# First stage of a two-layer diffusion block: one of two modulation vectors moved to fp32 matmuls on TensorE, the loads in a fixed order

## Chip, core and metric

The kernel runs on one core of one Trainium2 chip. The metric is the time of one execution on the device in microseconds. Each program is timed in several runs and the median counts.

## What is computed

The reference is a two-layer block on 512 latent tokens and 256 context tokens of width 1024: SwiGLU feed-forward, attention (windowed in layer 0, differential in layer 1) and a second feed-forward, each behind an RMS norm whose scale and shift come from a conditioning vector. The part that the change touches is the first norm of layer 0, with the modulation vectors it needs, and the first projections of the first feed-forward:

```python
def _rmsnorm(x, w):
    y = xf * lax.rsqrt(jnp.mean(xf * xf, axis=-1, keepdims=True) + EPS)
    return (y * w.astype(jnp.float32)).astype(x.dtype)

def _pre(h, gain, shift, scale):
    return _rmsnorm(h, gain) * (1.0 + scale) + shift

def _swiglu(h, w_gate, w_up, w_down):
    return (jax.nn.silu(h @ w_gate) * (h @ w_up)) @ w_down
...
mx = (silu_c @ ada_w[i] + ada_b[i]).reshape(B, N_MOD, 1, D)
mc = (silu_cc @ ada_w[i] + ada_b[i]).reshape(N_MOD, D)
fx = _swiglu(_pre(hx, norm_w[i, 0], mx[:, 0], mx[:, 1]), ...)
fc = _swiglu(_pre(hc, norm_w[i, 0], mc[0], mc[1]), ...)
```

The conditioning has two streams: `c` for the latent tokens and `c_ctx` for the context tokens. Of the nine modulation vectors of layer 0, number 0 is the shift and number 1 the scale of this first norm.

## The kernel before

**Layout.** Activations stand transposed in SBUF: `hT` is 8 slices (called d, or k when they are contracted over) of 128 features by 768 tokens. Each fp32 operand of a product is split in a high and a low fp32r part, and a product is three matmuls (high by high, low by high, high by low). `xh` and `xl` are the two parts of `hT` times the scale factor; `x_parts` (L187) makes them for one slice: ScalarE writes `xh` (L193) with the factor as its scale, VectorE writes `xl` (L194), each in a piece of 256 context tokens and one of 512 latent tokens. The two last columns of `xh` and `xl` hold the shift of the two streams, so that the projections of the shift come out as two more columns of the same matmul (386 columns instead of 384) and are added later as a bias. The norm's 1/rms is not multiplied in before the projections: `rstd` is applied to their results (`scaled`, L300). So the projections need the scale, the shift columns need the shift, and nothing needs `rstd` until the results are read.

**Modulation.** A block of 128 entries of a modulation vector is a product of 128 rows of the transposed `ada_w` with the conditioning. It is done on VectorE: one scalar_tensor_tensor over 128x1024 per stream, with the sum taken out through its accumulator (`ada_junk` is its unused result). `ada_fix` (L145) then adds the bias and, for a scale, one, and multiplies the norm's weight (L152, L153; L156 for a shift). The two conditioning rows lie spread over the 128 partitions in `s_bc`.

**The first stage**, `start` (L785), makes scale and shift for the eight slices, and the first three of the 44 projection units of the feed-forward (gate 0, up 0, gate 1; 128 outputs each, 48 matmuls a unit). Per slice it loads the factor rows of the scale and of the shift (512 KB each) and the slice of `hT` (384 KB). The scale's two products run on VectorE. Of the shift's sixteen products, four run on VectorE (L826) and twelve are multiplied on GpSimd (L823) and summed on ScalarE (L824). The squares of `hT` are made on ScalarE and summed over features by fp32 matmuls with a matrix of ones (`ssq`, L178), slice by slice, into a PSUM tile of their own, from which `norm` (L228) and `rsqrt` (L211) make `rstd`. Weights of a unit come from SyncE's queue into `w_raw`, ScalarE casts the high part (L815), GpSimd subtracts the low part (L816).

**What sets the order.** A scheduler puts the instructions of each engine into one fixed sequence when the program is built, by its own estimate of times; an engine then runs its own sequence strictly in turn and waits on semaphores. SyncE's queue issues the loads; at most eight are outstanding, since each waits for the one eight before it. The projection tiles come from the PSUM pool `pffn` (name `big`), which holds four tiles. Three belong to the first units, the fourth to the squares.

**After the stage** the feed-forward goes on with its other units and, beside them, with the remaining modulation vectors of the layer: 56 "side blocks" (`ada_block`, L123, its products on L131), two products each on VectorE, their rows in the same four `w_raw` buffers as the weights.

Of the kernel before, what the change touches and what calls it, by code (L numbers as in the profile page):

```python
# [10 lines left out]
F32 = mybir.dt.float32  # L11
F32R = mybir.dt.float32r
AF = mybir.ActivationFunctionType
ALU = mybir.AluOpType
# [3 lines left out]
P = 128  # L18
D = 1024
ND = D // P  # L20
SEQ = 512
CTX = 256
T = SEQ + CTX
# [11 lines left out]
class Net:  # L35
# [141 lines left out]

    def ssq(self, d, ps):  # L178

        nc = self.nc  # L180
        sq = self.tp.tile([P, T], F32, name="ta")
        nc.scalar.activation(out=sq, in_=self.hT[:, d], func=AF.Square)
        for i in range(2):
            nc.tensor.matmul(ps[:, i, :384], self.ones, sq[:, i * 384:(i + 1) * 384], start=(d == 0),
                             stop=(d == ND - 1))
# [599 lines left out]
    def start(self, pool):  # L785

        nc, a = self.nc, self.a
        wp = self.sb("w0", 3)
        rp = self.sb("ada_first", 6)
        units = []  # L790
        for which, i in ((0, 0), (1, 0), (0, 1)):
            hi = wp.tile([P, 1024], F32R, name="w0_hi")
            lo = wp.tile([P, 1024], F32R, name="w0_lo")
            units.append((hi, lo, a["ffn_gu"][0, 0, which, i], self.pbig.tile([P, 2, 512], F32, name="big")))
        ssq = self.pbig.tile([P, 2, 512], F32, name="big")

        def load(d):
            nc.sync.dma_start(self.hT[:, d], a["xT"][:, d])
            self.ssq(d, ssq)

        for d in range(3):
            load(d)
        for d in range(ND):
            raws = []
            for c in (1, 0):
                raw = rp.tile([P, D], F32, name="ada_raw0")
                nc.sync.dma_start(raw, a["ada_w"][0, c * 8 + d])
                raws.append(raw)
            if d + 3 < ND:
                load(d + 3)  # L810
            if d < 3:
                hi, lo, src, _ = units[d]
                raw = self.rawp.tile([P, 1024], F32, name="w_raw")
                nc.sync.dma_start(raw, src)
                nc.scalar.copy(out=hi, in_=raw)  # L815
                nc.gpsimd.tensor_tensor(out=lo, in0=raw, in1=hi.bitcast(F32), op=ALU.subtract)  # L816
            for c, raw in zip((1, 0), raws):
                b = c * 8 + d
                for s in range(2):
                    acc = self.mod[:, 0, s, b:b + 1]  # L820
                    junk = pool.tile([P, D], F32, name="ada_junk")
                    if c == 0 and (s == 1 or d % 2 == 1):
                        nc.gpsimd.tensor_tensor(out=junk, in0=raw, in1=self.sbc[:, s], op=ALU.mult)  # L823
                        nc.scalar.activation(out=junk, in_=junk, func=AF.Identity, accum_out=acc)  # L824
                    else:
                        nc.vector.scalar_tensor_tensor(out=junk, in0=raw, scalar=1.0, in1=self.sbc[:, s],  # L826
                                                       op0=ALU.mult, op1=ALU.mult, accum_out=acc)
                self.ada_fix(0, b)
            self.x_parts(0, 0, d)
            b = self.mod[:, 0, :, d]  # L830
            nc.vector.tensor_copy(out=self.xh[:, d, T:], in_=b)  # L831
            nc.vector.tensor_tensor(out=self.xl[:, d, T:], in0=b, in1=self.xh[:, d, T:].bitcast(F32),  # L832
                                    op=ALU.subtract)
        view = lambda t: t.rearrange("p (k m) -> p k m", m=P)
        us = [((view(hi), view(lo)), ps) for hi, lo, _, ps in units]
        for k in range(ND):
            self.project_k(us, (k,))
        rp.release()
# [264 lines left out]
```

## Time and profile before

| | us |
|---|---|
| median of 3 runs (2902.48 to 2910.11) | 2903.91 |
| the profiled execution | 2902.44 |
| its span, from first to last instruction | 2900.6 |
| TensorE busy in the span | 2770.0 |
| VectorE busy | 1555.9 |
| ScalarE busy | 972.4 |
| GpSimd busy | 1311.2 |
| granted TensorE clock, mean | 0.982 |

Times in the profile run from the start of the span. 1.84 us of the execution's time lie outside the span. PE is TensorE, PEld its weight loads, DVE VectorE, ACT ScalarE, POOL GpSimd, SP SyncE; a q behind a name is the sequencer, which issues loads. A row of the timeline has the start, the length, the engine, the line, the operation with its tiles and shape, the number of merged instructions, and in brackets how long the engine had been idle before and what released it. An fp32 matmul leaves two records each for its weight load and its product; an fp32r one leaves one.

### The profile page before, as it was taken

Reading aid. Unit: us, or ns where it says so; the run is one execution under the profiler, and the core shown is the slowest. Engines: PE = TensorE matmul, PEld = TensorE weight load, DVE = VectorE, ACT = ScalarE, POOL = GpSimd, SP = SyncE. Lnnn points to the kernel's source line nnn. Section 1 sums busy time; section 2 is a strip of 40 time slices with the busy share of each in tenths; the row PEclk is TensorE's granted clock in tenths of the full one; section 3 lists DMA queues with packets and bytes.
Section 4 is the critical chain, followed back from the end, with each engine's and each line's share of the span. In section 5 each row is a group of like instructions: output and inputs, shape, how many; then the busy total and the mean of one; then the engine's idle time right before and its main releaser. Section 6 shows DMA issues by size and latency. Waiting matters only on the chain. (4 is left out here: it accounts for less than half of the span.)

```text
span 2900.6 us, 40961 instructions
## 1 busy us (share of the span) xinstructions
PE 2770.0 (95%) x16150; PEld 2593.4 (89%) x16150; DVE 1555.9 (54%) x2683; ACT 972.4 (34%) x1749; POOL 1311.2 (45%) x762
## 2 busy tenths in 40 slices
PE   5899999999989899999999999999989999999998
PEld 3899999989877799999998999999988887799998
DVE  7955555567887544444447333344467678522223
ACT  4322122145666421221224212221345555422223
POOL 4443343355443443333335433333465665555553
PEclk7999999999999999999999999999999999999999
DMA  6333333333242323233223232232232333233331
GB/s 240 121 112 108 125 105 118 124 115 100 82 144 81 99 78 112 76 106 117 74 90 106 75 118 84 91 120 88 85 98 74 90 89 114 83 92 100 102 105 44
DMA packets 113423, 296.38 MB, mean 102 GB/s; under 512 B 12880, under 2 KB 30928, under 8 KB 113232
## 3 DMA queue, kind: packets, MB, share of 16 engines
q1 hardware_dynamic: 112944, 293.66, 31.8%
q8 instruction: 128, 2.10, 0.3%
q14 instruction: 63, 0.52, 0.1%
q10 hardware_dynamic: 288, 0.10, 0.0%
HBM read 260.42 MB, written 15.20 MB: 95 GB/s over the span
## 5 line engine op out<-in xcount | busy, mean ns | idle before, releaser
L56 POOL TENSOR_TENSOR w_lo<-w_raw,w_hi 128x1024 fp32r<-128x1024 f32 (+2 forms) x377 | 802.1, 2128 | 1072.1 <-ACT w_hi L55 1055.6
L266 PE MATMUL big<-xh,w_hi 128*128 128x384 f32 (+3 forms) x2816 | 696.6, 328 | 38.7 <-DVE xh L831 19.5
L55 ACT CAST w_hi<-w_raw 128x1024 fp32r<-128x1024 f32 (+2 forms) x377 | 337.4, 895 | 1132.6 <-PE big L70 394.1
L266 PE MATMUL big<-xl,w_hi 128*128 128x384 f32 (+3 forms) x2816 | 693.6, 327 | 8.3 <-DVE xl L832 5.0
L266 PE MATMUL big<-xh,w_lo 128*128 128x384 f32 (+3 forms) x2816 | 693.6, 328 | 2.3 <-POOL w_lo L56 2.3
L266 PEld LDWEIGHTS big<-xh,w_hi 128*128 128x128 f32 x2816 | 502.5, 191 | 47.2 <-DVE xh L831 22.3
L266 PEld LDWEIGHTS big<-xl,w_hi 128*128 128x128 f32 x2816 | 500.3, 191 | 10.5 <-DVE xl L832 6.3
L266 PEld LDWEIGHTS big<-xh,w_lo 128*128 128x128 f32 x2816 | 497.8, 190 | 3.8 <-POOL w_lo L56 3.3
L131 DVE SCALAR_TENSOR_TENSOR ada_junk<-w_raw,s_bc 128x1024 f32<-128x1024 f32 x224 | 342.4, 1546 | 291.6 <-DMA w_raw<-ada_w 290.4
L271 DVE COPY bias<-big 128x2 f32<-128x2 f32 x176 | 27.7, 157 | 621.1 <-PE big L266 620.9
L68 PE MATMUL big<-hh,w_hi 128*128 128x512 f32 (+1 forms) x1200 | 327.6, 344 | 0.0
L70 PE MATMUL big<-hl,w_hi 128*128 128x512 f32 (+1 forms) x1200 | 327.3, 344 | 0.0
L72 PE MATMUL big<-hh,w_lo 128*128 128x512 f32 (+1 forms) x1200 | 326.8, 344 | 0.0
L311 DVE SCALAR_TENSOR_TENSOR hT<-big,mod,hT 128x512 f32<-128x512 f32 (+1 forms) x288 | 167.6, 618 | 176.7 <-PE big L72 176.4
L70 PEld LDWEIGHTS big<-hl,w_hi 128*128 128x128 f32 x1200 | 226.1, 188 | 29.5
L72 PEld LDWEIGHTS big<-hh,w_lo 128*128 128x128 f32 x1200 | 225.0, 188 | 28.6
L68 PEld LDWEIGHTS big<-hh,w_hi 128*128 128x128 f32 x1200 | 224.9, 188 | 27.2
L966 POOL TENSOR_TENSOR hl<-tb,hh 128x768 fp32r<-128x768 f32 (+1 forms) x88 | 152.3, 1730 | 183.2 <-ACT hh L965 181.9
L961 DVE SCALAR_TENSOR_TENSOR tb<-tb,bias,ta 128x512 f32<-128x512 f32 (+1 forms) x154 | 176.1, 1177 | 8.7 <-DVE tb L304 0.5
L285 PE MATMUL half<-xh,w_hi 128*128 128x384 f32 (+3 forms) x464 | 155.5, 335 | 20.6 <-DVE ta L297 18.8
L965 ACT CAST hh<-tb 128x768 fp32r<-128x768 f32 (+1 forms) x88 | 68.7, 781 | 276.5 <-DVE tb L961 276.5
L285 PE MATMUL half<-xl,w_hi 128*128 128x384 f32 (+3 forms) x464 | 153.8, 331 | 0.0
(215 smaller groups left out, 3677.6 us busy)
## 6 DMA issues: line engine op xcount, KB each, us to landing
w_raw<-ffn_gu SPq DMA_DIRECT2D x176, 512.0 KB, 3.3
w_raw<-ada_w SPq DMA_DIRECT2D x128, 512.0 KB, 3.3
w_raw<-ffn_d SPq DMA_DIRECT2D x96, 256.0 KB, 2.7
w_raw<-ffn_d SPq DMA_DIRECT2D x64, 320.0 KB, 2.9
w_raw<-diff_in SPq DMA_DIRECT2D x24, 512.0 KB, 3.2
ada_raw<-ada_w SPq DMA_DIRECT2D x16, 512.0 KB, 7.2
w_raw<-gqa_in SPq DMA_DIRECT2D x12, 512.0 KB, 3.5
og<-god SPq DMA_DIRECT2D x6, 768.0 KB, 6.5
```

Source lines behind the costliest of these rows:

```text
L55: nc.scalar.copy(out=hi[:, :cols], in_=raw[:, :cols])
L56: nc.gpsimd.tensor_tensor(out=lo[:, :cols], in0=raw[:, :cols], in1=hi[:, :cols].bitcast(F32), op=ALU.subtract)
L68: nc.tensor.matmul(o, wh, xh, start=(k == 0), stop=False)
L70: nc.tensor.matmul(o, wh, xl, start=False, stop=False)
L72: nc.tensor.matmul(o, wl, xh, start=False, stop=(k == n - 1))
L131: getattr(nc, engines[s]).scalar_tensor_tensor(out=junk, in0=raw, scalar=1.0, in1=self.sbc[:, s], op0=ALU.mult, op1=ALU.mult, accum_out=se ...
L266: mm(ps[:, c, :e - s], w[:, k], x[:, k, s:e], start=first, stop=last)
L285: mm(ps[:, :e - s], w_[:, k], x[:, k, s:e], start=(k == 0 and i == 0), stop=(k == ND - 1 and i == 2))
L311: self.nc.vector.scalar_tensor_tensor(out=h, in0=o, scalar=self.mv(l, s, c, d), in1=h, op0=ALU.mult, op1=ALU.add)
L961: nc.vector.scalar_tensor_tensor(out=u[:, tk], in0=u[:, tk], scalar=bu[:, s:s + 1], in1=g[:, tk], op0=ALU.add, op1=ALU.mult)
L965: nc.scalar.copy(out=hh[:, toks], in_=u[:, toks])
L966: nc.gpsimd.tensor_tensor(out=hl[:, toks], in0=u[:, toks], in1=hh[:, toks].bitcast(F32), op=ALU.subtract)
```

## The change

- The shift no longer uses factor rows. `ada_w`'s columns of the shift come in their natural order as a new input `ada_k` (8 pieces of 128x1024), the conditioning as a 128x16 tile `s_cp`, and sixteen fp32 matmuls on TensorE (stationary 128x2, moving 128x512) sum the shift of both streams into a PSUM tile `shift` of 2x1024. ScalarE copies it out, eight small transposes turn it to 128 features by 2, VectorE adds the bias, and `x_bias` writes the shift columns of all eight slices at once. These matmuls, and all that depends on them, stand ahead of the first projections.
- GpSimd and ScalarE no longer take part in products of the first stage; the scale's sixteen products all stay on VectorE.
- The squares go slice by slice into `acc` on VectorE (7 additions of 128x768), and `norm` makes the sum over features with its own two matmuls, into a PSUM tile that it takes from the pool, as at the other feed-forwards.
- SyncE's loads in `start` stand in the order in which they are written (`manual_schedule`); the loads of `cos`, `sin` and `final_w` land in between.
- The pool with `ada_junk` has one buffer instead of two.

```diff
-        for which, i in ((0, 0), (1, 0), (0, 1)):
...
-        ssq = self.pbig.tile([P, 2, 512], F32, name="big")
...
+        scp = op.tile([P, ND, 2], F32, name="s_cp")
+        nc.scalar.dma_start(scp, a["cond_p"])
+        nc.scalar.activation(out=scp, in_=scp, func=AF.Silu)
+        shift = self.pbig.tile([P, 2, 512], F32, name="big")
+
+        def shift_part(k):
+            raw = kp.tile([P, D], F32, name="ada_rawk")
+            nc.sync.dma_start(raw, a["ada_k"][k])
+            for i in range(2):
+                nc.tensor.matmul(shift[:2, i], scp[:, k], raw[:, i * 512:(i + 1) * 512], start=(k == 0),
+                                 stop=(k == ND - 1))
...
+        with self.tc.manual_schedule(engines={nc.sync.engine}):
+            for d in range(ND):
+                raw = rp.tile([P, D], F32, name="ada_raw0")
+                nc.sync.dma_start(raw, a["ada_w"][0, ND + d])
+                nc.sync.dma_start(self.hT[:, d], a["xT"][:, d])
+                if d < 4:
+                    shift_part(2 * d)
+                    shift_part(2 * d + 1)
+                if d in (0, 2, 4):
+                    unit(d // 2 % 2, d // 4)
+                for s in range(2):
+                    junk = pool.tile([P, D], F32, name="ada_junk")
+                    nc.vector.scalar_tensor_tensor(out=junk, in0=raw, scalar=1.0, in1=self.sbc[:, s], op0=ALU.mult,
+                                                   op1=ALU.mult, accum_out=self.mod[:, 0, s, ND + d:ND + d + 1])
+                self.ada_fix(0, ND + d)
+                self.x_parts(0, 0, d)
+                sq = self.acc if d == 0 else self.tq.tile([P, T], F32, name="sq")
+                nc.scalar.activation(out=sq, in_=self.hT[:, d], func=AF.Square)
+                if d:
+                    nc.vector.tensor_tensor(out=self.acc, in0=sq, in1=self.acc, op=ALU.add)
+        row = op.tile([2, D], F32, name="shift_row")
+        nc.scalar.copy(out=row.rearrange("p (c n) -> p c n", c=2), in_=shift[:2])
+        turned = self.pbig.tile([P, 2, 512], F32, name="big")
...
+            nc.tensor.transpose(turned[:, 0, 2 * d:2 * d + 2], row[:, d * P:(d + 1) * P], self.ident[:2, :2])
+        nc.vector.tensor_tensor(out=self.mod[:, 0, :, 0:ND],
+                                in0=turned[:, 0, :2 * ND].rearrange("p (d s) -> p s d", s=2),
+                                in1=self.ada_b[:, 0:1, 0:ND].to_broadcast([P, 2, ND]), op=ALU.add)
+        self.x_bias(0, 0)
...
-        self.adap = self.sb("ada0", 2)
+        self.adap = self.sb("ada0", 1)
```

What it moves, in the sequences as built (line numbers of the changed program in the "now" pieces are its own: L809 and L792 are the loads of the factor rows and of `ada_k`, L818 the products of the scale, L185 is `xl`, L257 the projections, L230 the norm's matmuls, L210 the first reading of their result on VectorE). First SyncE's queue at its start, before: behind three slices of `hT` come pairs of factor rows (L807), with the slices and weights in turn.

```order
L120 DMA s_bc<-cond 128x1024 x2
L798 DMA hT<-xT 128x768 x3
L807 DMA ada_raw_146<-ada_w 128x1024
L807 DMA ada_raw_148<-ada_w 128x1024 [waits DMAHW0_49]
L798 DMA hT<-xT 128x768 [waits DMAHW1_49]
L814 DMA w_raw<-ffn_gu 128x1024 [waits DMAHW2_49]
L807 DMA ada_raw_177<-ada_w 128x1024 [waits DMAHW3_49]
L807 DMA ada_raw_179<-ada_w 128x1024 [waits DMAHW4_49]
```

And the same place now:

```order
L120 DMA s_bc<-cond 128x1024 x2
L809 DMA ada_raw_133<-ada_w 128x1024
L810 DMA hT<-xT 128x768
L792 DMA ada_rawk<-ada_k 128x1024
L792 DMA ada_rawk<-ada_k 128x1024 [waits DMAHW0_49]
L801 DMA w_raw<-ffn_gu 128x1024 [waits DMAHW1_49]
L809 DMA ada_raw_162<-ada_w 128x1024 [waits DMAHW2_49]
L810 DMA hT<-xT 128x768 [waits DMAHW3_49]
```

The first factor row moved ahead of the slices, and each slice is followed by two pieces of `ada_k` until all eight are issued. Second, VectorE where `rstd` is made. Before, the norm's four steps (L219, L221, L222, L223) stand in the middle of the stage, between products and fixes of the fourth and fifth slice:

```order
L826 SCALAR_TENSOR_TENSOR ada_junk,mod<-ada_raw_240,s_bc 128x1024
L219 TENSOR_SCALAR tb<-big 128x768 [waits Activation_49]
L152 TENSOR_SCALAR mod<-mod,ada_b 128x2 [waits DVE_49]
L221 TENSOR_TENSOR tb<-tb,ta 128x768 [waits DVE_49,Activation_49]
L153 TENSOR_SCALAR mod<-mod,norm_w 128x2 [waits DVE_49]
L222 SCALAR_TENSOR_TENSOR tb<-tb,ta 128x768 [waits DVE_49]
```

Now they stand at the stage's end, behind the last piece of `xl`, seven products of side blocks (L131) and the three copies of the bias columns, which wait for TensorE to finish the three units:

```order
L185 SCALAR_TENSOR_TENSOR xl<-hT,mod,xh 128x512 [waits Activation_49]
L131 SCALAR_TENSOR_TENSOR ada_junk,mod<-w_raw,s_bc 128x1024 [waits DVE_49]
L131 SCALAR_TENSOR_TENSOR ada_junk,mod<-w_raw,s_bc 128x1024 [waits DMAHW5_49,DVE_49]
L131 SCALAR_TENSOR_TENSOR ada_junk,mod<-w_raw,s_bc 128x1024 [waits DVE_49]
L131 SCALAR_TENSOR_TENSOR ada_junk,mod<-w_raw,s_bc 128x1024 [waits DMAHW7_49,DVE_49]
L262 COPY bias<-big 128x2 [waits PE_49] x2
L131 SCALAR_TENSOR_TENSOR ada_junk,mod<-w_raw,s_bc 128x1024 [waits DVE_49]
L262 COPY bias<-big 128x2 [waits PE_49]
L131 SCALAR_TENSOR_TENSOR ada_junk,mod<-w_raw,s_bc 128x1024 [waits DMAHW1_49,DVE_49]
L131 SCALAR_TENSOR_TENSOR ada_junk,mod<-w_raw,s_bc 128x1024 [waits DVE_49]
L210 TENSOR_SCALAR tb<-big 128x768 [waits Activation_49]
```

So the reading of the norm's sum (L210) moved behind seven side products counted from the last `xl`. Third, TensorE at the end of the first three units, now:

```order
L257 MATMUL big<-xh,w_lo 128x384
L257 MATMUL big<-xh,w_lo 128x386
L230 MATMUL big<-acc,ones 128x384 [waits PE_49]
L230 MATMUL big<-acc,ones 128x384
L257 MATMUL big<-xh,w_hi 128x384 [waits DVE_49]
L257 MATMUL big<-xh,w_hi 128x386
```

The two matmuls of the norm moved to the end of the stage, and the fourth unit behind them waits for VectorE: it takes the PSUM tile that the norm's sum stood in, and the step that gives it free is L210. Before, the fourth unit took the tile of the squares, which had been read long ahead. Behind this stage the sequences of all engines are those of before but for a few neighbours exchanged.

More of the change, by code (lines that the diff above doesn't have):

```diff
@@ L176, in x_bias @@
                                 op=ALU.subtract)
[L178 to L185, printed above, removed]
     def x_parts(self, l, n, d, xonly=False):
@@ L788, in start @@
         wp = self.sb("w0", 3)
-        rp = self.sb("ada_first", 6)
-        units = []
-        for which, i in ((0, 0), (1, 0), (0, 1)):
+        rp = self.sb("ada_first", 5)
+        kp = self.sb("ada_shift", 4)
+        op = self.sb("ada_one", 1)
+        scp = op.tile([P, ND, 2], F32, name="s_cp")
+        nc.scalar.dma_start(scp, a["cond_p"])
+        nc.scalar.activation(out=scp, in_=scp, func=AF.Silu)
+        units = []
+        shift = self.pbig.tile([P, 2, 512], F32, name="big")
[5 more added lines that the diff above has]
+                                 stop=(k == ND - 1))
@@ L792, in start, with unit @@
+        def unit(which, i):
             hi = wp.tile([P, 1024], F32R, name="w0_hi")
             lo = wp.tile([P, 1024], F32R, name="w0_lo")
-            units.append((hi, lo, a["ffn_gu"][0, 0, which, i], self.pbig.tile([P, 2, 512], F32, name="big")))
-        ssq = self.pbig.tile([P, 2, 512], F32, name="big")
[L797 to L802, printed above, removed]
-        for d in range(ND):
[L804 to L833, printed above, removed]
@@ new lines, in unit @@
+            w = self.rawp.tile([P, 1024], F32, name="w_raw")
+            nc.sync.dma_start(w, a["ffn_gu"][0, 0, which, i])
+            nc.scalar.copy(out=hi, in_=w)
+            nc.gpsimd.tensor_tensor(out=lo, in0=w, in1=hi.bitcast(F32), op=ALU.subtract)
+            units.append((hi, lo, None, self.pbig.tile([P, 2, 512], F32, name="big")))
+        with self.tc.manual_schedule(engines={nc.sync.engine}):
[18 more added lines that the diff above has]
+                    nc.vector.tensor_tensor(out=self.acc, in0=sq, in1=self.acc, op=ALU.add)
@@ L837, in start @@
             self.project_k(us, (k,))
+        op.release()
+        kp.release()
         rp.release()
         wp.release()
-        return {(0, 0): us[0][1], (1, 0): us[1][1], (0, 1): us[2][1]}, ssq
+        return {(0, 0): us[0][1], (1, 0): us[1][1], (0, 1): us[2][1]}, None
     def run(self):
@@ L1069, in pack @@
         "cond": np.stack([g["c"][0], g["c_ctx"]]),
+        "cond_p": np.stack([g["c"][0], g["c_ctx"]]).reshape(2, ND, P).transpose(2, 1, 0),
+        "ada_k": g["ada_w"][0, :, :D].reshape(ND, P, D),
         "ada_w": g["ada_w"].transpose(0, 2, 1).reshape(2, 72, P, D),
```

## Prediction

> **What bounds the kernel now.** I read the page first, then the busy times stage by stage, the waits of the first 100 us, the timeline of that stretch, and the groups of instructions in it. The page:
>
> ```profile
> PE 2770.0 (95%) x16150; PEld 2593.4 (89%) x16150; DVE 1555.9 (54%) x2683; ACT 972.4 (34%) x1749; POOL 1311.2 (45%) x762
> PE   5899999999989899999999999999989999999998
> DVE  7955555567887544444447333344467678522223
> ```
>
> TensorE is the bound nearly everywhere, except in the first slices of 72.5 us each, where it shows 5 and VectorE 7 and 9. So the first stage has a limit of its own. Its windows (busy time of PE, PEld, DVE, ACT, POOL, then granted clock, DMA share, GB/s):
>
> ```profile
> 0.00:20.00 20.00, 7.33 (x17) 3.87 (x17) 7.93 (x14) 9.03 (x11) 4.76 (x8) 0.98 0.93 347
> 20.00:40.00 20.00, 11.01 (x30) 6.96 (x30) 18.09 (x20) 8.07 (x13) 13.88 (x6) 0.67 0.87 340
> 40.00:62.25 22.25, 12.05 (x45) 9.21 (x44) 16.72 (x29) 11.46 (x17) 10.42 (x5) 0.73 0.36 118
> 62.25:102.94 40.69, 30.45 (x135) 28.10 (x136) 40.23 (x61) 12.65 (x22) 17.59 (x7) 0.84 0.24 78
> 110.00:150.00 40.00, 40.00 (x229) 40.00 (x228) 31.85 (x47) 11.67 (x15) 23.42 (x9) 1.00 0.44 144
> ```
>
> From 110 us TensorE has no gap. Up to 102.94 us, where the fourth unit starts, it works 60.8 us (7.33 + 11.01 + 12.05 + 30.45), much of it at a granted clock of 0.67 to 0.84, while VectorE is full from 62 us on (40.23 of 40.69) and the loads are idle by then (0.24). Who waits for whom up to 100 us:
>
> ```profile
> ACT xh L193 <- DVE mod L153: 29.2, 7, 7.1
> POOL ada_junk L823 <- DVE ada_junk L826: 22.5, 5, 12.8
> PE big L266 <- DVE xh L831: 19.5, 6, 6.7
> PE big L266 <- DVE xl L832: 5.0, 3, 2.8
> ```
>
> TensorE waits for VectorE's shift columns, ScalarE for VectorE's scale. Why VectorE is slow shows in the timeline:
>
> ```profile
> 12.78 1.22 DVE L826 SCALAR_TENSOR_TENSOR ada_junk<-ada_raw,s_bc 128x1024 f32<-128x1024 f32 x1
> 13.93 1.22 DVE L826 SCALAR_TENSOR_TENSOR ada_junk<-ada_raw,s_bc 128x1024 f32<-128x1024 f32 x1
> 14.09 3.25 POOL L823 TENSOR_TENSOR ada_junk<-ada_raw,s_bc 128x1024 f32<-128x1024 f32 x1 [12.79 <-DVE ada_junk L826]
> 15.07 2.30 DVE L152 TENSOR_SCALAR mod<-mod,ada_b 128x2 f32<-128x2 f32 x1
> 30.77 2.38 POOL L816 TENSOR_TENSOR w_lo<-w_raw,w_hi 128x1024 fp32r<-128x1024 f32 x1 [2.45 <-ACT w_hi L815]
> 50.31 0.96 DVE L219 TENSOR_SCALAR tb<-big 128x768 f32<-128x768 f32 x1 [3.13 <-ACT ta L218]
> ```
>
> GpSimd's product and VectorE's work shut each other out: L152 has two elements per partition and takes 2.30 us, up to the end of GpSimd's instruction, which itself waited for the product before it. L219, which reads PSUM, ran 0.96 us inside such a GpSimd span. Groups up to 103 us:
>
> ```profile
> L823 POOL TENSOR_TENSOR ada_junk<-ada_raw,s_bc 128x1024 f32<-128x1024 f32 x12 | 33.5, 2801 | 38.3 <-DVE ada_junk L826 22.5 <-issue 12.0 <-ACT ta L182 2.5
> L826 DVE SCALAR_TENSOR_TENSOR ada_junk<-ada_raw,s_bc 128x1024 f32<-128x1024 f32 x20 | 31.9, 1607 | 11.9 <-DMA ada_raw<-ada_w 10.6 <-ACT ada_junk L824 1.2
> L152 DVE TENSOR_SCALAR mod<-mod,ada_b 128x2 f32<-128x2 f32 x8 | 17.0, 2130 | 0.0
> ```
>
> **The change part by part.** What counts is when the fourth unit can start; behind it TensorE is continuous and the sequences hardly change. So the sum is that start, now 102.94 us, against the new one.
>
> *Removed from GpSimd:* the twelve products of L823, 33.5 us in which VectorE mostly stands still. Three w_lo subtractions (L816) and, before the end of the stage, two of the next units stay, 2.4 us each by the row at 30.77. *VectorE* loses 4 of 20 products and 24 small instructions of the shift, and gains 7 additions.
>
> *Loads.* Their landing is read here:
>
> ```profile
> 7.32 1.06 ACT L121 ACTIVATE s_bc<-s_bc 128x1024 f32<-128x1024 f32 x1 [0.36 <-DMA s_bc<-cond]
> 11.63 1.22 DVE L826 SCALAR_TENSOR_TENSOR ada_junk<-ada_raw,s_bc 128x1024 f32<-128x1024 f32 x1 [10.63 <-DMA ada_raw<-ada_w]
> 10.00:15.00 5.00, 5.00 (x13) 2.70 (x12) 3.37 (x5) 1.81 (x3) 0.91 (x1) 1.00 1.03 407
> ```
>
> `s_bc` (1.05 MB) has landed at 7.3; three slices and the first factor row (1.70 MB more) at 11.6, so 0.39 to 0.407 MB per us; I take 0.40. Counted along the new queue: first factor row 8.6, its slice 9.6, last piece of `ada_k` 30.9, third weights 34.5, last slice 41.4. The total hardly changes: eight factor rows against eight pieces of `ada_k`. The Trainium skill (SBUF — State Buffer, summary of rules) says to reckon with about 358 GB/s between HBM and SBUF; the window's 407 speaks against so low a figure here. By 358 the last slice would land near 45 and the sum below grow by about 1 us, since VectorE comes to that slice later still.
>
> *Shift on TensorE,* sixteen fp32 matmuls of 512 columns. The nearest rows are the fp32 matmuls of 384 columns, two records each:
>
> ```profile
> 10.01 0.34 PEld L184 LDWEIGHTS big<-ta,ones 128*128 128x128 f32 x1 [0.30 <-issue]
> 10.65 0.34 PEld L184 LDWEIGHTS big<-ta,ones 128*128 128x128 f32 x1 [0.30 <-issue]
> 46.55 1.45 PE L184 MATMUL big<-ta,ones 128*128 128x384 f32 x4
> 87.77 1.97 PE L266 MATMUL big<-xh,w_hi 128*128 128x386 f32 x5 [3.26 <-DVE xh L831]
> 91.13 0.52 PE L266 MATMUL big<-xh,w_lo 128*128 128x384 f32 x2
> 91.49 0.50 PE L266 MATMUL big<-xl,w_hi 128*128 128x384 f32 x2
> 102.94 0.98 PE L266 MATMUL big<-xh,w_hi 128*128 128x384 f32 x2
> ```
>
> Slow, 0.64 us a record (10.01 to 10.65), so 1.28 a matmul and 1.71 at 512 columns; fast, 1.45/2 = 0.73, or 0.97. All sixteen cost 15.5 to 27.3 us, mostly under the loads: with the last piece at 30.9 they end between 32.9 and 38.2 (no piece overtaken by loads; all slow without a gap from 10.9). ScalarE's copy of the result stands behind `xh` of slice 3, which is not made before 35.6 (below), so up to 35.6 they cost nothing and at worst 2.6 us. No row shows the copy or the transposes: copy 1.1 us (the PSUM read at 50.31 took 0.96), eight transposes 1.5 to 6 us (a weight load each, 0.19 us by the fast rows, or four of them); I take 1.9, so 38.7. In VectorE's sequence the reading of them stands behind the products of slice 4, which end at 38.7 too.
>
> *VectorE's chain.* Prices: product 1.2 us (1.15 from 12.78 to 13.93; 1.27 where `ada_junk` has one buffer, next rows), addition 0.9, the two fixes 0.33, the two pieces of `xl` 1.13 (rows of `mod` and `xl`: medians 0.22, 0.47 to 0.74, starts overlapping), hand-over to ScalarE and back 0.8.
>
> ```profile
> L194 DVE SCALAR_TENSOR_TENSOR xl<-hT,mod,xh x16: 470/610/2840, 18.2 to 89.0; 128x256 fp32r<-128x256 f32 x8, 128x512 fp32r<-128x512 f32 x8
> L153 DVE TENSOR_SCALAR mod<-mod,norm_w x8: 215/222/2273, 17.4 to 87.6; 128x2 f32<-128x2 f32 x8
> 1561.01 0.96 DVE L208 TENSOR_TENSOR acc<-sq,acc 128x768 f32<-128x768 f32 x1 [0.57 <-ACT sq L206]
> 1563.83 1.23 DVE L131 SCALAR_TENSOR_TENSOR ada_junk<-w_raw,s_bc 128x1024 f32<-128x1024 f32 x1 [1.20 <-DMA w_raw<-ada_w]
> 1565.10 3.29 DVE L131 SCALAR_TENSOR_TENSOR ada_junk<-w_raw,s_bc 128x1024 f32<-128x1024 f32 x1
> 1573.10 1.45 PE L239 MATMUL big<-acc,ones 128*128 128x384 f32 x4
> 1574.59 0.90 ACT L218 ACTIVATE ta<-big,eps 128x768 f32<-128x768 f32 x1 [0.56 <-PE big L239]
> 1575.53 0.96 DVE L219 TENSOR_SCALAR tb<-big 128x768 f32<-128x768 f32 x1 [2.07 <-ACT ta L218]
> ```
>
> Slice 0 from 8.7 (the second row of `s_bc` is through its Silu at 7.32 + 1.06) to 13.5. Slice 1 waits for its row (14.9) and the first w_lo, to 17.1. Slices 1 to 3 take 3 x 5.6 plus the second w_lo: 36.3. Two products of slice 4: 38.7. Third w_lo: 41.1. Addition, fixes, shift columns and a product: 43.9, the low shift columns. Then eight products, three additions, eight pieces of `xl`, the fixes and two w_lo of the next units: 9.6 + 2.7 + 4.5 + 1.0 + 4.8 = 22.6, so the last `xl` at 66.5. Then seven side products, three bias copies and L210: 8.4 + 0.45 + 0.96 = 9.8, so 76.3.
>
> *TensorE beside it.* Held by the shift columns until 43.9, it has 135 of 144 matmuls left, 0.177 us each at full speed (91.13 to 91.49 for two): 68.2, or 69.7 behind the last `xl` (66.5 + 18 x 0.177). Norm 1.45 and its Ln 0.90: 72.0. VectorE arrives 4 us later: it sets the start, 76.3.
>
> *The wait that is added.* The fourth unit waits for L210, and all of TensorE's sequence behind it. Idle from 71.1 to 76.3, TensorE starts slow again: after 3.26 us idle the matmuls at 87.77 needed about 2.4 us to reach full pace, some 1.2 us lost, and the old start lost about 0.7 (102.94, 0.98 for two). I take 1 to 2 us more than before. The Trainium skill (TensorE: Matmul & The Clock Gate, Part 1) has the clock halved after an idle window of about 3.4 us and restored after as long a busy one. By it an idle of 5.2 us costs 1.7 us; the row at 87.77 recovers sooner. The units after the fourth wait for `scaled` on the first results, which needs the rest of `rstd`: L210, three products, three steps and `scaled`, about 8.6 us behind L210; the fourth unit takes 48 x 0.177 = 8.5, so that is covered to within a microsecond. One buffer for `ada_junk` costs 0.07 to 0.12 us on each of the layer's 112 side products, on an engine with 8 of 40 us free (window 110 to 150): nothing; without that cover, up to 13 us.
>
> *Sum.* 102.94 - 76.3 = 26.6, less 1.6: 25 us. The profiled execution took 2902.44 (span 2900.6 and 1.84 outside): 2877.4. The median of the runs was 1.5 above it, so 2903.9 - 25 = 2879. A measurement of this kernel can tell about 0.3% (8.7 us) from no change.
>
> **The rivals.**
>
> *TensorE bounds the stage.* If VectorE is held up less (a w_lo slipping in where it is idle, side products not in the way of L210), the start is TensorE's: from 40 us 144 matmuls with a slow start, 68, norm, Ln and L210: 71. Gain 31 to 37. For it: VectorE's slack exists in slices 0 and 1. Against: the seven side products stand ahead of L210 in the sequence.
>
> *VectorE is held up more.* The 27 products cost 1.6 instead of 1.2, as the mean of L826 (1607 ns) with all its lock-outs: 11 us more, gain 14, or 10 to 19. For it: GpSimd still has five w_lo. Against: twelve of its instructions are gone.
>
> *TensorE stays slow.* Fed in small pieces it would do the 135 matmuls at half pace (0.32): from 46 to 90, the fourth unit at 95, gain 7. For it: granted clocks of 0.67 to 0.84 up to 102 us, with gaps. Against: from 44 us on four slices are ready and more come faster than they are used; from 110 on the clock is 1.00. The Trainium skill's page on TensorE (HAM oscillation) describes bursts that never get warm because each wait is longer than the window.
>
> *The shift's matmuls are the bound, and it gets slower.* All first projections stand behind them. At p us per matmul they end at 10.9 + 16p, and the fourth unit starts some 40 us later (copy, transposes, shift columns, 25.6 us of matmuls at full pace, norm). This passes 102.94 at p = 3.3 and loses over 8.7 us from p = 3.8 on; at 4 it gives 115, so 2916. For it: no row shows a 2-column stationary with a 512-column fp32 stream. Against: the columns streamed set the nearest rows, and they give 0.97 to 1.71.
>
> *It is given back later.* The gain stays if the rest is bound by TensorE at the same pace; a rest that waits elsewhere for VectorE or loads could eat it. Busy 9 in nearly all slices speaks against. Time 2901 to 2904.
>
> **How the numbers follow.** Forecast (gain 19 to 31) 0.60; TensorE bounds 0.14; VectorE held up more 0.13; slow TensorE 0.05; given back 0.03; shift bound 0.05. The range leaves out the last two and the slow end of the slow TensorE: gains of 38 to 11, 2866 to 2893. Faster by over 0.3%: 0.60 + 0.14 + 0.13 and half of the slow case, 0.90; same 0.05; slower 0.05.
>
> **What would show it.** Right: no GpSimd product in the first stage, L152 at 0.22 us; last shift matmul between 33 and 38 us; last `xl` near 66; one gap of TensorE of about 5 us ended by L210; the fourth unit's start near 76; from there no gap. Wrong: shift matmuls over 2 us each; gaps of TensorE waiting for each slice; a granted clock near 0.5 from 45 to 70 us; a later stage longer than before.

## The result and the profile after

| | before | changed |
|---|---|---|
| median of 4 runs, us | 2903.2 (2902.48 to 2910.11) | 2885.31 (2883.55 to 2886.75) |
| ratio, 95% interval | 1 | 0.9938 (0.9926 to 0.9951) |
| profiled execution, us | 2902.44 | 2884.58 |
| its span, us | 2900.6 | 2882.8 |

Faster by 17.9 us, where 25 was forecast. The page of the changed kernel, same lines as shown of before:

```profile
PE 2765.0 (96%) x16162; PEld 2583.7 (90%) x16162; DVE 1523.9 (53%) x2661; ACT 962.3 (33%) x1727; POOL 1274.4 (44%) x750
PE   6999999999998899999999999999989999999998
DVE  8645455567886744445446333334468677522223
```

TensorE's second slice (72 to 144 us) went from 8 to 9 tenths, its first from 5 to 6. The windows of the first stage (columns as before: PE, PEld, DVE, ACT, POOL, granted clock, DMA share, GB/s):

```profile
0.00:20.00 20.00, 9.27 (x16) 1.43 (x16) 9.84 (x17) 7.46 (x9) 3.05 (x7) 1.00 0.91 345
20.00:40.00 20.00, 10.77 (x28) 2.42 (x27) 17.71 (x27) 8.35 (x12) 5.81 (x2) 0.90 1.03 407
40.00:62.25 22.25, 21.13 (x107) 21.13 (x108) 22.25 (x41) 7.75 (x12) 3.58 (x2) 0.86 0.34 126
62.25:83.25 21.00, 17.68 (x88) 16.80 (x87) 20.86 (x34) 7.89 (x9) 2.39 (x1) 0.92 0.59 181
```

GpSimd's busy time from 0 to 62 us fell from 29.06 to 12.44 us, and from 40 to 62 us TensorE is nearly full (21.13 of 22.25 us). The groups of instructions up to 83 us:

```profile
L818 DVE SCALAR_TENSOR_TENSOR ada_junk<-ada_raw,s_bc 128x1024 f32<-128x1024 f32 x16 | 23.6, 1476 | 8.6 <-DMA ada_raw<-ada_w 8.4
L794 PE MATMUL big<-ada_rawk,s_cp 128*2 128x512 f32 x32 | 18.4, 730 | 15.9 <-DMA ada_rawk<-ada_k 15.8
L152 DVE TENSOR_SCALAR mod<-mod,ada_b 128x2 f32<-128x2 f32 x8 | 1.8, 224 | 0.0
```

L152, eight instructions of two elements per partition, fell from 17.0 us to 1.8. The shift costs TensorE 18.4 us (two records a matmul). The chain in order of time, rows chosen from the timeline:

```profile
8.36 1.22 DVE L818 SCALAR_TENSOR_TENSOR ada_junk<-ada_raw,s_bc 128x1024 f32<-128x1024 f32 x1 [7.36 <-DMA ada_raw<-ada_w]
...
29.03 5.29 PE L794 MATMUL big<-ada_rawk,s_cp 128*2 128x512 f32 x8 [2.51 <-DMA ada_rawk<-ada_k]
34.55 0.98 ACT L827 COPY shift_row<-big 2x1024 f32<-2x1024 f32 x1
35.68 0.62 PE L830 MATMUL big<-ident,shift_row 2*128 2x2 f32 x8 [1.36 <-ACT shift_row L827]
37.30 2.73 POOL L803 TENSOR_TENSOR w_lo<-w_raw,w_hi 128x1024 fp32r<-128x1024 f32 x1 [6.17 <-ACT w_hi L802]
37.76 0.17 DVE L831 TENSOR_TENSOR mod<-big,ada_b 128x16 f32<-128x16 f32 x1
40.90 0.16 DVE L174 CAST xh<-mod 128x16 fp32r<-128x16 f32 x1
41.12 0.69 PE L257 MATMUL big<-xh,w_hi 128*128 128x386 f32 x1 [3.40 <-DVE xh L174]
42.30 0.17 DVE L175 TENSOR_TENSOR xl<-mod,xh 128x16 fp32r<-128x16 f32 x1
...
60.66 0.74 DVE L185 SCALAR_TENSOR_TENSOR xl<-hT,mod,xh 128x512 fp32r<-128x512 f32 x1
65.11 3.32 DVE L131 SCALAR_TENSOR_TENSOR ada_junk<-w_raw,s_bc 128x1024 f32<-128x1024 f32 x1
68.41 1.45 PE L230 MATMUL big<-acc,ones 128*128 128x384 f32 x4
72.18 0.95 DVE L210 TENSOR_SCALAR tb<-big 128x768 f32<-128x768 f32 x1
73.19 0.81 PE L257 MATMUL big<-xh,w_hi 128*128 128x384 f32 x2 [3.32 <-DVE tb L210]
```

TensorE gets the shift columns at 41 us and runs without a gap to the norm; the one gap behind it, 3.32 us, is ended by L210, and the fourth unit starts at 73.19.

That row must not be set against before's row at 102.94. The projection matmuls of before up to 102.9 us, by form:

```profile
L266 PE MATMUL big<-xh,w_hi 128*128 128x386 f32 x32 | 13.3, 428 | 19.5 <-DVE xh L831 19.5
...
L266 PE MATMUL big<-xh,w_hi 128*128 128x384 f32 x32 | 11.3, 404 | 6.0 <-ACT xh L193 6.0
```

Six forms with 32 each are 192 matmuls, four units of 48. Before had woven the fourth unit into its first stage, and at 102.94 the **fifth** starts. The changed kernel starts its fifth unit (its 193rd matmul) at 83.25: 19.7 us earlier. The gain at later places, from the first matmul of the norm there: 22.3 us at the attention block's norm (639.5 against 617.2), 16.6 at the next norm behind that block (1006.1 against 989.5), 17.8 at the end.

### The profile page after: what moved, and what is told of

Same layout as the page of the kernel before. It is cut to its first block, busy times and chain, and to the rows that moved or that the text cites. A ratio compares the mean times of both kernels' runs of the same rounds, so it can differ in the third digit from the quotient of the medians.

```text
span 2882.8 us, 40921 instructions
## 1 busy us (share of the span) xinstructions
PE 2765.0 (96%) x16162; PEld 2583.7 (90%) x16162; DVE 1523.9 (53%) x2661; ACT 962.3 (33%) x1727; POOL 1274.4 (44%) x750
## 5 line engine op out<-in xcount | busy, mean ns | idle before, releaser
L257 PE MATMUL big<-xh,w_hi 128*128 128x384 f32 (+3 forms) x2816 | 691.9, 327 | 22.4 <-DVE hT L302 13.1
L257 PE MATMUL big<-xl,w_hi 128*128 128x384 f32 (+3 forms) x2816 | 689.4, 326 | 3.3 <-DVE xl L185 3.2
L257 PE MATMUL big<-xh,w_lo 128*128 128x384 f32 (+3 forms) x2816 | 690.9, 327 | 0.4 <-POOL w_lo L56 0.4
L257 PEld LDWEIGHTS big<-xh,w_hi 128*128 128x128 f32 x2816 | 501.0, 191 | 26.7 <-ACT sq L197 11.1
L257 PEld LDWEIGHTS big<-xl,w_hi 128*128 128x128 f32 x2816 | 498.7, 190 | 4.1 <-DVE xl L185 4.1
L257 PEld LDWEIGHTS big<-xh,w_lo 128*128 128x128 f32 x2816 | 496.9, 190 | 0.8 <-POOL w_lo L56 0.8
L131 DVE SCALAR_TENSOR_TENSOR ada_junk<-w_raw,s_bc 128x1024 f32<-128x1024 f32 x224 | 330.1, 1474 | 304.5 <-DMA w_raw<-ada_w 302.3
```

Of the source, the lines that this page charges most:

```text
L131: getattr(nc, engines[s]).scalar_tensor_tensor(out=junk, in0=raw, scalar=1.0, in1=self.sbc[:, s], op0=ALU.mult, op1=ALU.mult, accum_out=se ...
L257: mm(ps[:, c, :e - s], w[:, k], x[:, k, s:e], start=first, stop=last)
```

## The experiments

The theories. **A:** GpSimd's twelve products shut VectorE out, and taking them away is the gain. **B:** it is the fixed order of loads. **C:** it is that TensorE makes all shift columns at once. Then the price of the wait for L210, and where 5.7 us went between two norms.

"Fifth unit" is the start of the 193rd projection matmul in the profiled run; "block" the stretch from the attention block's norm to the next norm; the ratio is to before on the same chip.

| run | fifth unit, us | block, us | span, us | median, us | ratio (95%) |
|---|---|---|---|---|---|
| before | 102.94 | 366.6 | 2900.6 | 2903.2 | 1 |
| changed | 83.25 | 372.3 | 2882.8 | 2885.31 | 0.9938 (0.9926 to 0.9951) |
| e1 before, fixed loads | 102.41 | 370.0 | 2901.9 | 2906.46 | 1.0024 (1.0015 to 1.0033) |
| e2 before, VectorE only | 86.29 | 370.9 | 2886.2 | 2890.66 | 0.9973 (0.9963 to 0.9983) |
| e3 both of these | 84.80 | 373.7 | 2892.2 | 2888.80 | 0.9965 (0.9953 to 0.9978) |
| e4 changed, free loads | 93.74 | 370.8 | 2891.9 | 2894.98 | 0.9983 (0.9974 to 0.9991) |
| e5 changed again | 83.03 | 372.7 | 2883.3 | 2886.63 | 0.9944 (0.9931 to 0.9956) |
| e6 changed, GpSimd products added | 108.34 | 369.9 | 2904.6 | 2908.07 | 1.0025 (1.0016 to 1.0034) |
| e7 changed, norm ahead | 78.43 | 369.3 | 2876.2 | 2879.34 | 0.9924 (0.9911 to 0.9938) |
| e8 changed, x tokens first | 83.75 | 359.7 | 2870.1 | 2872.04 | 0.9902 (0.9888 to 0.9915) |
| e9 e7 and e8 | 78.14 | 359.1 | 2869.8 | 2870.52 | 0.9892 (0.9877 to 0.9908) |
| e10 changed, shift twice | 86.51 | 373.8 | 2888.5 | 2887.86 | 0.9954 (0.9942 to 0.9967) |
| e11 e2 with x tokens first | 87.64 | 360.3 | 2879.8 | 2877.70 | 0.9920 (0.9907 to 0.9934) |
| e12 before, x tokens first | 102.25 | 357.8 | 2892.2 | 2895.18 | 0.9983 (0.9974 to 0.9992) |

In the comparisons of e1 to e12 before's median was 2900.1 to 2901.4. The two profiles of the changed kernel (changed, e5) differ by 0.2 us at the fifth unit and 0.5 at the end, so a stage can be read from one profile, as far as this one pair tells; single whole executions differ by more (e3's profiled run ended 8.4 us before before's, its median 11.3 below).

**e1.** The first stage of before with its loads in program order.

```
+        with self.tc.manual_schedule(engines={nc.sync.engine}):
             for d in range(3):
                 load(d)
             for d in range(ND):
...
```

> The kernel before with one edit: SyncE's loads of the first stage stand in program order; all else is left to the scheduler. Theory A (the gain comes from taking GpSimd's twelve products away, which shut VectorE out): the loads were idle from 62 us on while VectorE was full, so nothing much changes: time within 4 us of before (2899 to 2907), GpSimd's products still 33 us in sum, the scale fix L152's mean still about 2.1 us. Theory B (the gain comes from the order of the loads): 9 to 18 us faster than before (2885 to 2894). Theory C (the gain comes from having all shift columns at once from TensorE): no change either, as by A.

The stage is as it was (102.41), GpSimd's products take 34.1 us in sum and L152 2062 ns, as A had it. The time is 6.3 us (0.24%) longer, more than the 4 that A allowed; in the profiled run 3.4 us went in the attention block. By itself, the order of loads gives before nothing; B falls for the old kernel.

**e2.** All 32 products of the old stage on VectorE.

```
-                    if c == 0 and (s == 1 or d % 2 == 1):
+                    if False:
```

> The kernel before with one edit: the twelve products that GpSimd made (and ScalarE summed) are made on VectorE like the other twenty; the shift still comes from natural weights, loads by the scheduler. Theory A: VectorE takes on 12 x 1.2 = 14.4 us and is no longer shut out for 33.5 us of GpSimd products; of these about two thirds counted, so 8 us faster (4 to 14: 2889 to 2899), L152 at 0.22 us. Theory B: no change (within 4 us). Theory C: TensorE still gets its shift columns slice by slice, behind 32 products of VectorE instead of 20, so 0 to 14 us slower.

Groups up to 103 us of this run:

```profile
L826 DVE SCALAR_TENSOR_TENSOR ada_junk<-ada_raw,s_bc 128x1024 f32<-128x1024 f32 x32 | 38.3, 1213 | 10.3 <-DMA ada_raw<-ada_w 10.3
L152 DVE TENSOR_SCALAR mod<-mod,ada_b 128x2 f32<-128x2 f32 x8 | 1.7, 216 | 0.0
```

VectorE makes twelve products more and is done earlier: they cost 38.3 - 31.9 = 6.4 us, and L152 alone gives 15.3 back. The fifth unit starts 16.7 us earlier, 85% of the change's 19.7, by one line. A holds, and was even too modest for the stage; C falls. The whole gains less than the stage: 7.8 us by the ratio (0.9973), 9.5 by the medians, 14.4 by the spans of the profiled runs; its executions lie between 2887.55 and 2895.85. In the profiled run 4.3 us went in the attention block.

**e3.** Both edits.

> The kernel before with both edits: all products on VectorE, and SyncE's loads in program order. Theory A: as the run with the first edit alone, within 4 us of it. Theory B: as the run with fixed loads alone, 9 to 18 us faster than before. Theory C: 0 to 14 us slower than before.

The fifth unit comes 1.5 us earlier than in e2; the ratios of e2 and e3 can't be told apart. As A had it.

**e4.** The changed kernel, loads left to the scheduler.

```
-        with self.tc.manual_schedule(engines={nc.sync.engine}):
-            for d in range(ND):
+        for d in range(ND):
...
```

> The changed kernel with one edit: SyncE's loads are left to the scheduler. Theories A and C: within 4 us of the changed kernel (2881 to 2889). Theory B: the gain is lost, 2894 to 2904.

Here B is right and A and C are wrong. SyncE's queue, the shift's matmuls and ScalarE's copy in this run, rows chosen:

```profile
20.42 2.88 SPq L809 DMA_DIRECT2D hT<-xT  x3
24.00 0.33 SPq L792 DMA_DIRECT2D ada_rawk<-ada_k  x1
25.24 0.33 SPq L106 DMA_DIRECT2D cos<-cos  x1
...
28.79 1.34 SPq L126 DMA_DIRECT2D w_raw<-ada_w  x2
30.78 0.33 SPq L792 DMA_DIRECT2D ada_rawk<-ada_k  x1
33.03 3.57 PE L794 MATMUL big<-ada_rawk,s_cp 128*2 128x512 f32 x4 [12.52 <-DMA ada_rawk<-ada_k]
33.05 1.00 SPq L792 DMA_DIRECT2D ada_rawk<-ada_k  x2
38.29 6.97 PE L794 MATMUL big<-ada_rawk,s_cp 128*2 128x512 f32 x12 [1.69 <-DMA ada_rawk<-ada_k]
...
50.50 0.98 ACT L826 COPY shift_row<-big 2x1024 f32<-2x1024 f32 x1
```

The scheduler puts four pieces of `ada_k` behind three token slices; three of them also behind `cos`, `sin`, `final_w` and two factor rows of a later stage. The last shift matmul ends at 45.3 instead of 34.3, the copy stands at 50.5 instead of 34.55, the fifth unit starts 10.5 us later. The time lies in B's range and keeps 0.17% against before. So the order of loads is no gain of its own, but a condition of the new shift: with the shift on TensorE, all first projections stand behind the last piece.

**e5.** The changed kernel unedited.

> The changed kernel once more, unedited, as the comparison for the three runs beside it. All theories: ratio to before 0.993 to 0.995, the fifth unit at 82 to 84 us of its profile.

As expected: 83.03, 0.9944.

**e6.** GpSimd's products given back.

```
+                    if s == 1 or d % 2 == 1:
+                        dum = op.tile([P, D], F32, name="ada_dummy")
+                        nc.gpsimd.tensor_tensor(out=dum, in0=raw, in1=self.sbc[:, s], op=ALU.mult)
-        kp = self.sb("ada_shift", 4)
+        kp = self.sb("ada_shift", 3)
```

> The changed kernel with twelve GpSimd products of 128x1024 added (each factor row times the same broadcast rows, into a tile that nobody reads; one buffer less for the pieces of ada_k). It gives back GpSimd's share of the old first stage and nothing else. Theory A (these products shut VectorE out): about 12 x 2.8 = 33 us of GpSimd work return, of which about half falls on VectorE's path, so the fifth unit starts 10 to 22 us later than in the changed kernel (93 to 105) and the time is 10 to 20 us longer. Theory C (the gain is the shift columns from TensorE): VectorE is slower but TensorE is fed from 41 to 46 us on as before, so at most 5 us longer.

The groups up to 103 us:

```profile
L822 POOL TENSOR_TENSOR ada_dummy<-ada_raw,s_bc 128x1024 f32<-128x1024 f32 x12 | 35.1, 2926 | 7.5 <-DMA ada_raw<-ada_w 6.9
L818 DVE SCALAR_TENSOR_TENSOR ada_junk<-ada_raw,s_bc 128x1024 f32<-128x1024 f32 x16 | 27.7, 1728 | 7.4 <-DMA ada_raw<-ada_w 7.1
L152 DVE TENSOR_SCALAR mod<-mod,ada_b 128x2 f32<-128x2 f32 x8 | 8.0, 1000 | 0.0
```

And from the timeline the last matmuls of the shift and the copy of it on ScalarE:

```profile
28.80 3.60 PE L794 MATMUL big<-ada_rawk,s_cp 128*2 128x512 f32 x8 [2.51 <-DMA ada_rawk<-ada_k]
47.91 0.98 ACT L830 COPY shift_row<-big 2x1024 f32<-2x1024 f32 x1
```

The products' results are used nowhere, yet the fifth unit comes 25.1 us later and the time is 21 us longer (2908.07 against 2886.63 beside it): slower than before. L152 and L818 are long again, and through ScalarE's queue even the copy of the shift, which VectorE does not make, comes 13 us later. Above A's 10 to 22, far above C's 5. Two other causes fall by these rows: the buffer that the edit takes from `ada_k` did not hold the shift up, since its matmuls end at 32.4 us here and at 34.3 without the products, and L818 waits for loads 7.1 us in all, not more than the 8.4 there. The copy stands behind an `xh` that waits 11.2 us for VectorE's L153. With e2 this shows A from both sides.

**e7.** The norm's matmuls ahead of the last slice.

```
         for k in range(ND):
+            if k == ND - 1:
+                self.norm()
             self.project_k(us, (k,))
...
-        self.norm(xonly, ssq)
+        if not first:
+            self.norm(xonly, ssq)
```

> The changed kernel with the norm's two matmuls placed ahead of the last slice's projections (they need only the squares' sum, which is ready by then), so that the Ln and L210 run beside TensorE's last projections. If TensorE's wait of 3.32 us for L210 and the slow restart behind it (12 matmuls at 0.32 instead of 0.177, 1.7 us) are what the added wait costs: the gap is gone, the fourth unit starts near 70 instead of 73.2, the fifth near 78.5 instead of 83.25, and the time is 4.5 us shorter (3 to 6). Rival (the wait only moves, to the units that need rstd): less than 1.5 us shorter.

```profile
65.49 1.45 PE L230 MATMUL big<-acc,ones 128*128 128x384 f32 x4
...
69.96 0.51 PE L257 MATMUL big<-xh,w_hi 128*128 128x384 f32 x2
```

No gap and no slow restart: the fourth unit starts at 69.96, the fifth at 78.43, 4.8 earlier, and the granted clock is 1.00 from 60 us to there. That is what the added wait cost in the stage. The time is 7.3 us below e5's, 6.6 by the spans, above the 3 to 6 expected, and not all of it is this wait: of the 4.8 us 3.4 are left at the attention block's norm (613.9 against 617.2), and 3.0 come from the attention block, which the edit does not touch (369.3 against 372.3).

**e8.** An edit 850 us behind the change, in the attention block's out_proj.

```
-            for part in (((0, 1, 2, 3),) if len(units) == 1 else ((0, 1), (2, 3))):
+            for part, js in ((((0, 1, 2, 3), (0, 1)),) if len(units) == 1 else
+                             (((0, 1), (0, 1)), ((2, 3), (1,)), ((2, 3), (0,)))):
...
-                            for ps, (s, tk) in zip(outs, cuts):
+                            for j in js:
...
-                    if part[-1] == 3:
+                    if part[-1] == 3 and 0 in js:
```

> The changed kernel with one edit 930 us later, at the end of the attention block: the first out_proj that uses the last group's reloaded output takes the 512 columns of the x tokens for all four row blocks first, the 256 columns of the context, whose reload lands last, behind them. In before the scheduler had put six of those matmuls ahead of TensorE's wait for that reload (wait 2.31 us), in the changed kernel none (5.14 us). Theory (the loss of 5.6 us between the attention block's norm and the next is this order): the wait falls from 5.14 to under 1 us and the stretch from norm to norm from 372.3 to 366 to 369 us. Rival (the loss is elsewhere in that stretch): the wait goes but the stretch stays within 1.5 us of 372.

The two waits of TensorE at the end of the block, of before, of the changed kernel and of this run:

```profile
950.71 0.40 PE L520 MATMUL half<-og,w_lo 128*128 128x512 f32 x1
953.41 1.33 PE L520 MATMUL half<-og,w_hi 128*128 128x256 f32 x5 [2.31 <-DMA og<-god]
...
986.80 0.98 PE L266 MATMUL big<-xh,w_hi 128*128 128x384 f32 x2 [8.20 <-DVE hT L311]
```

```profile
926.40 0.52 PE L511 MATMUL half<-og,w_lo 128*128 128x256 f32 x2
932.05 1.76 PE L511 MATMUL half<-og,w_hi 128*128 128x256 f32 x4 [5.14 <-DMA og<-god]
...
970.79 0.98 PE L257 MATMUL big<-xh,w_hi 128*128 128x384 f32 x2 [10.76 <-DVE hT L302]
```

```profile
959.06 0.98 PE L257 MATMUL big<-xh,w_hi 128*128 128x384 f32 x2 [4.61 <-DVE hT L302]
```

The third fence is e8's; its wait for the reload is no longer there. The changed kernel waits 2.8 us longer for the reload and 2.6 longer for the last residual: 5.4 of the 5.7 us. The scheduler plans the whole program anew for every edit, and had put matmuls of 512 columns ahead of the wait in before and none in the changed kernel. With them first, the wait for the reload is gone, and the wait for the last residual is more than halved: the block takes 359.7 us, below the 366 to 369 expected. Why that second wait shrank is not shown. VectorE's last rows ahead of it, first of the changed kernel, then of e8:

```profile
959.35 2.37 DVE L131 SCALAR_TENSOR_TENSOR ada_junk<-w_raw,s_bc 128x1024 f32<-128x1024 f32 x1
...
963.58 1.21 DVE L131 SCALAR_TENSOR_TENSOR ada_junk<-w_raw,s_bc 128x1024 f32<-128x1024 f32 x1
...
966.92 1.13 DVE L302 SCALAR_TENSOR_TENSOR hT<-half,mod,hT 128x256 f32<-128x256 f32 x2
...
969.50 1.14 DVE L302 SCALAR_TENSOR_TENSOR hT<-half,mod,hT 128x256 f32<-128x256 f32 x2
```

```profile
951.93 3.23 DVE L131 SCALAR_TENSOR_TENSOR ada_junk<-w_raw,s_bc 128x1024 f32<-128x1024 f32 x1
...
958.44 1.14 DVE L302 SCALAR_TENSOR_TENSOR hT<-half,mod,hT 128x256 f32<-128x256 f32 x2
```

Products for a later stage stand ahead of the last residuals in both (e8 has a second one of 1.21 us at 957.29), so they alone do not make the difference. When TensorE has done the out_proj (960.0 us, 954.5 in e8), VectorE still has two pairs of residuals to make in the changed kernel and one in e8.

**e9.** e7 and e8 together.

> The changed kernel with both later edits: the norm's matmuls ahead of the last slice's projections, and the x tokens first in the attention block's out_proj. If the two remove separate waits (the first was 6.6 us shorter by its span, the second 12.9), the sum is 19 us: 2862 to 2868, ratio to before 0.986 to 0.9885, the fifth unit at 77 to 79. If they overlap: 2869 to 2873.

Both waits are gone in the trace (fifth unit 78.14, block 359.1), but the time is that of the second expectation: 2870.5, 1.5 us below e8, and the intervals of the two ratios overlap. Of the 5.6 us won at the fifth unit against e8, 1.6 are left at the attention block's norm. A wait for a `w_lo` of GpSimd that e8 does not have, 2.32 us at 132, and one that grew from 0.31 to 0.58 us at 606 make up 2.6 of those 4.0 us; the rest I did not find. It has the lowest median of the study, 1.1% below before.

**e10.** Every shift matmul twice.

```
-            for i in range(2):
-                nc.tensor.matmul(shift[:2, i], scp[:, k], raw[:, i * 512:(i + 1) * 512], start=(k == 0),
-                                 stop=(k == ND - 1))
+            for rep in range(2):
+                for i in range(2):
+                    nc.tensor.matmul(shift[:2, i], scp[:, k], raw[:, i * 512:(i + 1) * 512],
+                                     start=(k == 0 and rep == 0), stop=(k == ND - 1 and rep == 1))
```

> The changed kernel with each of the shift's sixteen matmuls made twice (the copy halves the sum, so the result stands). It asks whether the shift on TensorE is on the path. In the changed kernel the sixteen took 18.4 us between 10.7 and 34.3. Thirty-two at 0.86 to 1.71 us end between 43 and 60. As the prediction had it (VectorE sets the start of the fourth unit, TensorE has 4 us to spare), the fifth unit starts 5 to 20 us later. Rival (the shift has room to spare under the loads): under 2 us later.

Rows chosen from the timeline:

```profile
10.55 29.27 PE L795 MATMUL big<-ada_rawk,s_cp 128*2 128x512 f32 x64 [10.55 <-DMA ada_rawk<-ada_k]
48.85 0.69 PE L257 MATMUL big<-xh,w_hi 128*128 128x386 f32 x1 [3.10 <-DVE xh L174]
50.94 2.82 PE L230 MATMUL big<-acc,ones 128*128 128x384 f32 x4
```

Thirty-two matmuls take 29.3 us, 0.91 each without a wait, and end at 39.8, earlier than any of my bounds. The projections with shift columns start 7.7 us later (48.85 against 41.12), the fifth unit only 3.3: the scheduler now puts the norm (50.94) among the projections, and the wait for L210 is gone. Neither expectation holds in its size. The shift is on the path in the sense of the first, but with some 4 us of the L210 wait to lose.

**e11.** e2 with the out_proj of e8.

> The kernel before with the twelve products on VectorE and the x tokens first in the attention block's out_proj: no shift on TensorE, no fixed loads. If the shift on TensorE and the fixed loads are worth only the 2 us that their first stages differ by (fifth unit at 84.7 with VectorE alone, 82.5 in the changed kernel), it comes within 4 us of the changed kernel with the same out_proj: ratio 0.989 to 0.993, about 2870 to 2880. If they carry the gain: ratio above 0.995.

The ratio, 0.9920, lies in the upper half of the range given, but the median is 5.7 us behind e8's, not within 4. (The first stages of e2 and the changed kernel differ by 3.0 us, 86.29 against 83.25, and not by 2.) Compared at the same out_proj, the shift on TensorE and the fixed loads are worth 3.9 us at the fifth unit (87.64 against 83.75) and 5 to 6 in the whole by ratios and medians; the intervals of the two ratios overlap, so the second figure is uncertain.

**e12.** Before with the out_proj of e8.

> The kernel before with one edit: the x tokens first in the attention block's out_proj. If the edit only removes the wait for the reload, it saves the 2.3 us that before waits there and up to 3 us at the end of the block, 2 to 5 us in all (ratio 0.998 to 0.9993), against 12.9 in the changed kernel. If it is worth as much here as there (10 us or more, ratio under 0.9966), the order of out_proj was a loss of before as well, and not one that the change brought.

5.5 us less (2.3 to 7.5 by the interval): at the upper end of the first expectation; the block fell by 8.8 us, 2.3 of which are lost again behind it. In the changed kernel the same edit gave 14.6. So the order of out_proj was a loss in before too, and a larger one in the changed kernel. With this out_proj the one line of e2 can be priced with the block nearly equal (357.8, 360.3 and 359.7 us): from e12 to e11 it gains 17.5 us (2895.18 to 2877.70), and the whole change, from e12 to e8, about 23 by the ratios. By these figures the one line is about three quarters of the gain.

## Why the prediction was right, and where it was not

**What bounds the stage** (right, and shown by e2 and e6). GpSimd's and VectorE's instructions hold each other up, and VectorE held TensorE up. The Trainium skill (SBUF — State Buffer, Who interferes with whom) calls the port pair that the two share an exclusive lock held for a whole instruction; L152 at 2130 ns beside the products, 224 without them and 1000 in e6 agrees.

**Loads** (right). First product at 8.36 us for a row forecast at 8.6, 407 GB/s from 20 to 40 us, the shift's last matmul at 34.3 in 32.9 to 38.2. That nothing overtakes the pieces was the condition, and e4 shows its price: 10.5 us.

**Shift on TensorE** (right in its bounds): 18.4 us in 15.5 to 27.3, the copy 0.98 for 1.1. The eight transposes took 0.62 us, below the 1.5 to 6 given.

**VectorE's chain** (right in kind, 3.1 us too long). Low shift columns at 42.5 for 43.9; last `xl` at 61.4 for 66.5. Of these 5.1 us 1.4 were there at the shift columns, and 2.4 are a w_lo that did not fall ahead of the last `xl` but among the seven side products (3.32 at 65.11), which took the last part from 9.8 to 11.7; the rest is spread over the small terms. L210 ends at 73.1 for 76.3.

**TensorE beside it** (right to 1.3 us): 68.41 for 69.7. (43.9 + 135 x 0.177 is 67.8 and not 68.2, which changes nothing, as the last `xl` set the end.) The start, 73.2, fell between the forecast's 76.3 and the 71 of the rival in which TensorE bounds the stage.

**The wait that is added** (right). 3.32 us idle where 5.2 was forecast, then 12 matmuls at 0.32 us instead of 0.177, 1.7 lost. The Trainium skill (TensorE: Matmul & The Clock Gate, Part 1) has the clock halved after an idle window of about 3.4 us and restored after about 3.4 us of work. 12 x 0.32 = 3.8 us, at a granted clock of 0.55 from 73.2 to 77 us, agrees with the second, better than the row at 87.77 that I preferred; the idle of 3.32 us was a little under the window that the Trainium skill names, and the restart was slow all the same. e7 measures the wait and the restart together: 4.8 us in the stage.

**The sum** (wrong by one unit). "What counts is when the fourth unit can start" was set against 102.94, which is the fifth unit's start in before. I counted the units of the code, not the matmuls of the trace, which the groups by form give: 192. The miscount is 48 x 0.177 = 8.5 us too much gain. Corrected, the forecast's own terms give the fifth unit at 76.3 + 12 x 0.32 + 36 x 0.177 = 86.5, a gain of 16.4 at that place; measured 19.7.

**"Behind it TensorE is continuous and the sequences hardly change"** (wrong). From 73.2 us to the attention block's norm TensorE has no gap over 0.5 us, but the sequences changed everywhere, and not only by a few neighbours exchanged, as I had read them before: 2.6 us were won in that ffn (two waits for `w_lo` of before, 1.83 us at 478 and 0.86 at 630, are gone), 5.7 lost in the attention block, 1.2 won again behind it. I gave "given back later" 0.03 with a price of the whole gain; a part of it happened. A later stage longer than before was one of my signs of being wrong, and it came.

So 25 - 8.5 (unit) + 3.1 (VectorE earlier) + 0.1 (restart and rounding) - 1.9 (later stages) = 17.8, the difference of the spans. Two errors of opposite sign hid the miscount in part: the sign and the mechanism were right, the size by less than it looks.

**Which case came** (the band that the number fell in is chance). 17.9 us is below the 19 to 31 of the forecast's own case and lies in the 10 to 19 that I gave to "VectorE is held up more". That rival's mechanism did not come: VectorE was done 3.1 us before the forecast. L818's mean of 1476 ns, against 1.2 us, comes from the w_lo that the sum has as terms of their own: two of its sixteen products took 3.2 us beside one, at 14.42 and 28.96, the others 1.22 or 1.23. That TensorE stays slow did not come either: its granted clock was 0.50 from 41 to 46 us and 1.00 from 46 to 69.

## What to carry to other kernels

An instruction moved to an idle GpSimd need not be free while VectorE works on operands in SBUF: here twelve products moved from GpSimd to VectorE made VectorE's products 6.4 us longer and the fifth unit 16.7 us earlier. Price what such an instruction holds VectorE up by, and try the one-line edit that moves it back before a larger rewrite. When two traces are compared at a mark, count the matmuls ahead of it in both, since a scheduler may have moved work across it. Where a scheduler plans the whole program, look at the fragile waits far from the edit, too; here one order of matmuls 850 us later was worth nearly as much as the change.

## What the runs showed of the hardware that was not expected

- An fp32 matmul with a stationary of two columns streamed 512 columns in 0.91 us (e10, 29.27 us for 32): no dearer by the column than the ones with 128 columns (0.73 us for 384).
- Eight transposes of two rows took 0.62 us in all, 0.08 each, though each loads weights.
- Twelve GpSimd products whose results nobody reads (35.1 us) delayed TensorE's fifth unit by 25.1 us: in this kernel about 70% of GpSimd's busy time came through to the path.
